# MLP's first slice: weight sums on VectorE fed by GpSimd's DMA queue, the relu's square on ScalarE

## The chip, the cores and the metric

One Trainium2 chip, one core. The metric is the device time of one execution in microseconds. Times quoted as "median" come from three executions; every profile line comes from one profiled execution.

## The reference

One layer of a streaming encoder trunk on 528 tokens (16 meta tokens and 512 of the sequence) of width 1024, all in float32. An input projection feeds a recurrent branch and an attention branch; both are gated, merged and added to `h`. Then follows the part that matters here, on the 512 tokens that are returned:

```python
z = rmsnorm(h, norm_mlp[l])
h = h + (jnp.square(jax.nn.relu(z @ w_up[l])) @ w_down[l])
return h[:, N_META:]
```

`w_up` is 1024 x 4096 and `w_down` 4096 x 1024.

## The kernel before, in words

**Precision.** TensorE multiplies in a reduced float32 format. Each operand is split in a high part (a cast, on ScalarE) and a low part (operand minus high part, on VectorE), and a product is three matmuls: high x high, high x low, low x high (`passes`). So every weight piece that comes from memory (tile `wraw`, 128x512) costs a cast to `whi` on ScalarE and a subtraction to `wlo` on VectorE before TensorE can use it. For the up weights that is `load_h` (L231 the load, L234 the cast, L235 the low part); for the down weights it is `fill`, through `split` (L269, L270). `wraw`, `whi` and `wlo` have four buffers each.

**The MLP.** It starts at 553.7 us of the span. The 4096 hidden units are cut in 32 blocks of 128 and these in four slices of eight blocks. A slice has two stages:

1. The up stage (L1220 to L1236). For each of the eight blocks, 24 matmuls make `po` in PSUM, 128 hidden units by 512 tokens (L1143). `up_evac` takes it out: ScalarE writes relu(po) to `r` (L1149), and VectorE multiplies max(po, 0) by `r` into two of the 256-token columns of `R` (L1150). After every second block, `left_factors` makes the seven left factors of a Strassen-Winograd product from `R`: three subtractions and additions (L1160, L1161, L1162), casts to `fhi` on ScalarE (L1155) and low parts `flo` on VectorE (L1156). Then `factor_sums` makes four sums of down-weight pieces for this pair.
2. The product stage (L1285 to L1309). Seven products (L1256) of left factors with right factors follow. The right factors are plain quarters of `w_down` (B11, B21, B22) or sums of them (T1 to T4). The order of `FACTORS` is B11, B21, T4, T2, T3, T1, B22, so the first sum is read in the third product.

The first slice differs in that the first three blocks' first halves of tokens are multiplied early (`held`), while the last tokens of `z` are still being made.

**The sums.** `factor_sums(p0, j)` loads four pieces of 128x512 (b11, b12, b22, b21) with `quarter`, into the tile `traw` of three buffers, on SyncE's DMA queue (L1176). GpSimd adds them (L1184): T1 = b11 + b12, T3 = b12 + b22, T2 = T1 + b22, T4 = T2 + b21. A slice has 16 such sums, four for each of its four pairs, in tiles `t` that live until that slice's product has read them. SyncE's queue also carries the up weights (L231) and the plain down-weight pieces (also L1176, into `wraw`); it issues in order, and an issue waits until its buffer is free.

**What sets the order.** In the MLP the order of each engine's instructions, and of each DMA queue, is set when the program is built: a scheduler keeps a time for each engine and takes the earliest-written instruction that is ready by its own model. On the chip each engine follows its list in order and waits where an operand is not there.

Of the kernel before, what the change touches and what calls it, by code (L numbers as in the profile page):

```python
# [13 lines left out]
AF = mybir.ActivationFunctionType  # L14
ALU = mybir.AluOpType
# [171 lines left out]
def kernel(ctx, tc, ht, x, win, par, cst, gain, lora, wout, wo, wup, wdn, out, dbg=None):  # L187
    nc = tc.nc
    dbg = dbg or {}
    mm = nc.tensor.matmul  # L190
    act = nc.scalar.activation
    V, G, A = nc.vector, nc.gpsimd, nc.scalar
# [45 lines left out]
    def load_w(src, low=(V, V)):  # L238

        return [load_h(src[:, 512 * j:512 * j + 512], low[j], "w", (4, 4, 4)) for j in range(2)]  # L240
# [31 lines left out]
    def passes(w, x):  # L272
        return ((w[0], x[0]), (w[0], x[1]), (w[1], x[0]))
# [3 lines left out]
    quarters = [[wdn[i][256 * c:256 * c + 256] for c in range(8)] for i in range(4)]  # L277
# [761 lines left out]
    def ppo():  # L1039
        return ps.tile([128, 512], F32, name="po")  # L1040
# [4 lines left out]
    with ExitStack() as st:  # L1045
# [7 lines left out]
        for m in range(KB):  # L1053
            w = load_w(wout[m])
            pp = []
            for br in range(2):
# [3 lines left out]
                po = ppo()  # L1060
# [21 lines left out]
        for j in range(2):  # L1082
            we = yp.tile([128, 2, 2, 512], F32R, name=f"we{j}", tag=("y_rw", "y_fx")[j])
            for x in range(2):
                raw = wp.tile([128, 512], F32, name="wraw", bufs=4)
# [11 lines left out]
        for k in range(KB):  # L1097
            raw = wp.tile([128, 512], F32, name="wraw", bufs=4)
# [9 lines left out]
        for i in range(4):  # L1108
            po = ppo()
# [26 lines left out]
    with ExitStack() as st:  # L1136
        dp = st.enter_context(tc.tile_pool(name="dp", bufs=1))

        def up_part(w, po, t0, t1):
            n = 0  # L1140
            for k in range(KB):
                for a, b in passes(wk(w, k), Z):
                    mm(po[:, t0:t1], a, b[:, k, t0:t1], start=n == 0, stop=n == 23)  # L1143
                    n += 1

        def up_evac(po, out):

            r = dp.tile([128, 512], F32, name="r", bufs=2)
            act(r, po, AF.Relu)  # L1149
            V.scalar_tensor_tensor(out, po.rearrange("p (a b) -> p a b", b=256), 0.0, r.rearrange("p (a b) -> p a b", b=256), ALU.max, ALU.mult)  # L1150

        def left_factors(fhi, flo, j, R):

# [12 lines left out]
        B11, B12, B22, B21, T1, T2, T3, T4 = range(8)  # L1166
# [4 lines left out]

        sums = {}

        def quarter(right, pair, pool=dp, name="traw", bufs=3):
            raw = pool.tile([128, 512], F32, name=name, bufs=bufs)
            nc.sync.dma_start(raw, quarters[right][pair // 2][128 * (pair % 2):128 * (pair % 2) + 128])  # L1176
            return raw

        def factor_sums(p0, j):
            pair = p0 + j  # L1180
            b11, b12, b22, b21 = (quarter(x, pair) for x in (B11, B12, B22, B21))
            for x, c, d in (T1, b11, b12), (T3, b12, b22), (T2, T1, b22), (T4, T2, b21):
                t = dp.tile([128, 512], F32, name=f"t{x}{j}")
                G.tensor_tensor(t, sums[c, pair] if c in (T1, T2) else c, d, ALU.add)  # L1184
                sums[x, pair] = t

        def right_factor(right, pair):
            return sums[right, pair] if (right, pair) in sums else quarter(right, pair, wp, "wraw", 4)

        def fill(n):  # L1190

            while line and len(ready) < n:
                right, p, j = line.pop(0)
                raw = right_factor(right, p + j)
                hi = wp.tile([128, 512], F32R, name="whi", bufs=4)
                lo = wp.tile([128, 512], F32R, name="wlo", bufs=4)
                split(hi, lo, raw)
                ready.append((hi, lo))
# [7 lines left out]
        def soon(*jobs):  # L1206
            later.extend(jobs)

        for p0, n_pairs in zip(FIRST, SLICES):
            fhi = dp.tile([128, max(SLICES), 7, 256], F32R, name="fhi")  # L1210
            flo = dp.tile([128, max(SLICES), 7, 256], F32R, name="flo")
            blocks = list(range(2 * p0, 2 * (p0 + n_pairs)))
            held, R = [], None
            if p0 == 0:

                ws, pos = early + [load_w(wup[2])], [ppo() for i in range(3)]
                for w, po in zip(ws, pos):
                    up_part(w, po, 0, 256)
                held = list(zip(ws, pos))
            for n, b_ in enumerate(blocks):  # L1220
                if held:
                    w, po = held.pop(0)
                    up_part(w, po, 256, 512)
                else:
                    w = load_w(wup[b_])
                    po = ppo()
                    up_part(w, po, 0, 512)
                if n == 2 * n_pairs - 1:
                    fill(AHEAD)
                if n % 2 == 0:  # L1230
                    R = yp.tile([128, 8, 256], F32, name="R", tag=("y_rw", "y_fx")[n // 2 % 2])
                    up_evac(po, R[:, 0:8:7, :])
                else:
                    up_evac(po, R[:, 1:3, :])
                    left_factors(fhi, flo, n // 2, R)
                    factor_sums(p0, n // 2)  # L1236

            first, last = p0 == 0, p0 + n_pairs == 16

            def product(x, left, start, stop, end=False):  # L1240

                for j in range(n_pairs):
                    fill(1)
                    w = ready.pop(0)
                    if later:
                        later.pop(0)()
                    if end and j >= n_pairs - 2:
                        if j == n_pairs - 2:
                            held = w
                            continue  # L1250
                        order = [(i, j + d, (held, w)[d + 1]) for i in range(2) for d in (-1, 0)]
                    else:
                        order = [(i, j, w) for i in range(2)]
                    for i, k, u in order:
                        for n, (a, c) in enumerate(passes((fhi, flo), u)):
                            mm(x[i], a[:, k, left, 128 * i:128 * i + 128], c, start=start and k == 0 and n == 0,  # L1256
                               stop=stop and k == n_pairs - 1 and n == 2)

            def own(left, end=False):
                x = [ppo() for i in range(2)]  # L1260
                product(x, left, True, True, end)
                return x

            def gathered(v, left):
                for i, x in enumerate(own(left)):
                    if first:
                        A.copy(v[:, i], x)
                    else:
                        V.tensor_tensor(v[:, i], v[:, i], x, ALU.add)

            def add(a, b, i, x, op):
                h = hr[a][b][:, i]
                V.tensor_tensor(h, h, x, op)  # L1273

            def store(a, b, i):
                r0 = 256 * a + 128 * i
                nc.sync.dma_start(out[r0:r0 + 128, 512 * b:512 * b + 512], hr[a][b][:, i])

            def added(a, b, left, op, end=False):
                for i, x in enumerate(own(left, end)):  # L1280
                    add(a, b, i, x, op)
                    if end:
                        store(a, b, i)

            gathered(v1, A11)  # L1285
            added(0, 0, A12, ALU.add)
            if last:
                for i in range(2):
                    soon(lambda i=i: (add(0, 0, i, v1[:, i], ALU.add), store(0, 0, i)))
            added(1, 0, A22, ALU.add)  # L1290
            product(x6, S2, first, last)
            if last:
                for i in range(2):
                    V.tensor_tensor(v1[:, i], x6[i], v1[:, i], ALU.subtract)
                    soon(lambda i=i: add(0, 1, i, v1[:, i], ALU.add))
            product(x7, S3, first, last)
            if last:
                for i in range(2):
                    V.tensor_tensor(v1[:, i], v1[:, i], x7[i], ALU.subtract)
                    soon(lambda i=i: (add(1, 0, i, v1[:, i], ALU.subtract), store(1, 0, i)))  # L1300
                for i in range(2):
                    soon(lambda i=i: add(1, 1, i, v1[:, i], ALU.add))
            gathered(v5, S1)
            if last:
                for i in range(2):
                    soon(lambda i=i: add(0, 1, i, v5[:, i], ALU.subtract))
                for i in range(2):
                    soon(lambda i=i: (add(1, 1, i, v5[:, i], ALU.subtract), store(1, 1, i)))
            added(0, 1, S4, ALU.subtract, last)  # L1309
# [77 lines left out]
```

## Time and profile before

| | |
|---|---|
| median of 3 runs | 893.23 us (890.7 to 898.81) |
| profiled execution | 891.46 us, span 889.7 us |
| mean granted TensorE clock | 0.987 |
| up stage of the first slice | 553.7 to 601.4 us |
| its first product stage | from 601.4 us |
| GpSimd's busy time over the span | 246.0 us, in 201 instructions |

A row of a group reads: line, engine, operation, output <- inputs, shapes, count; then busy time and the mean of one in ns; then the engine's idle time before them and what ended it. A row of waits reads: who waited, for whom, us in total, number of times, the longest. A row by windows gives the busy time of each engine and its number of instructions in that stretch, then the granted TensorE clock, the share of the DMA engines and GB/s. A row of the timeline gives start, duration and, in brackets, the engine's idle time before it and what ended it. PE is TensorE, PEld its weight loads, DVE VectorE, ACT ScalarE, POOL GpSimd, SP SyncE; SPq is SyncE's queue of DMA issues.

### The profile page before, as it was taken

Reading aid. Unit: us, or ns where it says so; the run is one execution under the profiler, and the core shown is the slowest. Engines: PE = TensorE matmul, PEld = TensorE weight load, DVE = VectorE, ACT = ScalarE, POOL = GpSimd, SP = SyncE. Lnnn points to the kernel's source line nnn. Section 1 sums busy time; section 2 is a strip of 40 time slices with the busy share of each in tenths; the row PEclk is TensorE's granted clock in tenths of the full one; section 3 lists DMA queues with packets and bytes.
Section 4 is the critical chain, followed back from the end, with each engine's and each line's share of the span. In section 5 each row is a group of like instructions: output and inputs, shape, how many; then the busy total and the mean of one; then the engine's idle time right before and its main releaser. Section 6 shows DMA issues by size and latency. Waiting matters only on the chain. (4 is left out here: it accounts for less than half of the span.)

```text
span 889.7 us, 15657 instructions
## 1 busy us (share of the span) xinstructions
PE 855.4 (96%) x5896; PEld 697.0 (78%) x5896; DVE 632.1 (71%) x1178; ACT 447.9 (50%) x927; POOL 246.0 (28%) x201
## 2 busy tenths in 40 slices
PE   7889899999999999999979999999999999999998
PEld 6878887778896787677758778978888888888886
DVE  6975896547878883565467655598687768877787
ACT  7747333865465533664464553246445434543552
POOL 1154443222353351112102200550640152046000
PEclk9999999999999999999979999999999999999999
DMA  6121114021121241212266550463564175326431
GB/s 215 52 93 48 49 39 150 2 89 56 51 65 52 65 137 56 78 50 72 65 220 196 183 180 11 131 193 91 171 209 108 51 230 159 118 70 226 117 97 71
DMA packets 52363, 95.90 MB, mean 108 GB/s; under 512 B 5816, under 2 KB 6968, under 8 KB 52288
## 3 DMA queue, kind: packets, MB, share of 16 engines
q1 hardware_dynamic: 49984, 90.71, 33.0%
q10 hardware_dynamic: 2304, 4.20, 1.3%
q8 instruction: 46, 0.75, 0.4%
q14 instruction: 29, 0.24, 0.1%
HBM read 88.57 MB, written 6.31 MB: 107 GB/s over the span
## 5 line engine op out<-in xcount | busy, mean ns | idle before, releaser
L497 PE MATMUL pj<-uhi,whi 128*128 128x264 f32 (+1 forms) x480 | 167.3, 348 | 0.0
L497 PE MATMUL pj<-ulo,whi 128*128 128x264 f32 (+1 forms) x480 | 155.6, 324 | 2.4 <-DVE ulo L400 2.4
L467 POOL TENSOR_TENSOR wlo<-wraw,whi 128x512 fp32r<-128x512 f32 x76 | 104.7, 1381 | 191.4 <-ACT whi L466 175.0
L497 PE MATMUL pj<-uhi,wlo 128*128 128x264 f32 (+1 forms) x480 | 155.2, 323 | 0.0
L497 PEld LDWEIGHTS pj<-uhi,whi 128*128 128x128 f32 x480 | 91.4, 191 | 20.4 <-issue 11.3
L1184 POOL TENSOR_TENSOR t<-traw 128x512 f32<-128x512 f32 x32 | 47.0, 1478 | 209.1 <-DVE wlo L270 132.0
L497 PEld LDWEIGHTS pj<-ulo,whi 128*128 128x128 f32 x480 | 91.8, 191 | 7.2 <-DVE ulo L400 2.9
L497 PEld LDWEIGHTS pj<-uhi,wlo 128*128 128x128 f32 x480 | 91.6, 191 | 7.1
L1143 PE MATMUL po<-zhi,wlo 128*128 128x512 f32 (+1 forms) x248 | 95.0, 383 | 1.6 <-DVE wlo L235 1.6
L235 DVE TENSOR_TENSOR wlo<-wraw,whi 128x512 fp32r<-128x512 f32 x88 | 75.8, 874 | 27.7 <-ACT whi L234 27.7
L1143 PE MATMUL po<-zhi,whi 128*128 128x512 f32 (+1 forms) x248 | 94.8, 382 | 0.0
L1143 PE MATMUL po<-zlo,whi 128*128 128x512 f32 (+1 forms) x248 | 94.8, 382 | 0.0
L234 ACT CAST whi<-wraw 128x512 fp32r<-128x512 f32 x88 | 53.5, 618 | 46.3 <-DMA wraw<-in_wup 27.8
L466 ACT CAST whi<-wraw 128x512 fp32r<-128x512 f32 x80 | 49.0, 619 | 41.3 <-PE pj L497 21.0
L1256 PE MATMUL po<-wlo,fhi 128*128 128x512 f32 x160 | 62.8, 392 | 0.2 <-DVE wlo L270 0.2
L1256 PE MATMUL po<-whi,flo 128*128 128x512 f32 x160 | 62.5, 390 | 0.0
L270 DVE TENSOR_TENSOR wlo<-t,whi 128x512 fp32r<-128x512 f32 x64 | 49.3, 784 | 18.5 <-ACT whi L269 17.6
L269 ACT CAST whi<-t 128x512 fp32r<-128x512 f32 x64 | 40.0, 625 | 44.1 <-DVE wlo L270 19.8
L1256 PE MATMUL po<-whi,fhi 128*128 128x512 f32 x160 | 62.0, 389 | 0.0
L1143 PEld LDWEIGHTS po<-zhi,wlo 128*128 128x128 f32 x248 | 46.6, 188 | 11.4 <-DVE wlo L235 2.4
L1143 PEld LDWEIGHTS po<-zlo,whi 128*128 128x128 f32 x248 | 46.6, 188 | 9.1
L1143 PEld LDWEIGHTS po<-zhi,whi 128*128 128x128 f32 x248 | 46.6, 188 | 8.9
(294 smaller groups left out, 1842.2 us busy)
## 6 DMA issues: line engine op xcount, KB each, us to landing
wraw<-in_win SPq DMA_DIRECT2D x84, 256.0 KB, 2.8
wraw<-in_wup SPq DMA_DIRECT2D x64, 256.0 KB, 3.6
traw<-in_wdn SPq DMA_DIRECT2D x64, 256.0 KB, 3.0
wraw<-in_wdn SPq DMA_DIRECT2D x48, 256.0 KB, 2.7
gd<-gt ACTq DMA_DIRECT2D x16, 256.0 KB, 2.0
wraw<-in_wout SPq DMA_DIRECT2D x16, 256.0 KB, 3.1
gl<-gd SPq DMA_DIRECT2D x16, 256.0 KB, 3.0
wraw<-in_wo SPq DMA_DIRECT2D x16, 256.0 KB, 3.0
```

The lines of the kernel that those rows point to most:

```text
L234: A.copy(hi, raw)
L235: low.tensor_tensor(lo, raw, hi.bitcast(F32), ALU.subtract)
L269: A.copy(hi, x)
L270: V.tensor_tensor(lo, x, hi.bitcast(F32), ALU.subtract)
L466: A.copy(hi, raw)
L467: low.tensor_tensor(lo, raw, hi.bitcast(F32), ALU.subtract)
L497: mm(po, a, b[:, k, a0:a1], start=n == 0, stop=n == 23)
L1143: mm(po[:, t0:t1], a, b[:, k, t0:t1], start=n == 0, stop=n == 23)
L1184: G.tensor_tensor(t, sums[c, pair] if c in (T1, T2) else c, d, ALU.add)
L1256: mm(x[i], a[:, k, left, 128 * i:128 * i + 128], c, start=start and k == 0 and n == 0, stop=stop and k == n_pairs - 1 and n == 2)
```

## The change

Only the first slice (`p0 == 0`) is touched, in three ways. Its 16 sums run on VectorE instead of GpSimd. The 16 pieces they read are issued by GpSimd's DMA queue instead of SyncE's; they still share the three `traw` buffers, which slices two to four go on filling from SyncE's queue and reading with GpSimd. And the square in its eight `up_evac` calls is ScalarE's `Square` of `r`, instead of VectorE's product of max(po, 0) with `r`. The values computed are the same.

```diff
-        def up_evac(po, out):
+        def up_evac(po, out, by_act):
 
             r = dp.tile([128, 512], F32, name="r", bufs=2)
             act(r, po, AF.Relu)
-            V.scalar_tensor_tensor(out, po.rearrange("p (a b) -> p a b", b=256), 0.0, r.rearrange("p (a b) -> p a b", b=256), ALU.max, ALU.mult)
+            r = r.rearrange("p (a b) -> p a b", b=256)
+            if by_act:
+                act(out, r, AF.Square)
+            else:
+                V.scalar_tensor_tensor(out, po.rearrange("p (a b) -> p a b", b=256), 0.0, r, ALU.max, ALU.mult)
...
-        def quarter(right, pair, pool=dp, name="traw", bufs=3):
+        def quarter(right, pair, pool=dp, name="traw", bufs=3, queue=nc.sync):
             raw = pool.tile([128, 512], F32, name=name, bufs=bufs)
-            nc.sync.dma_start(raw, quarters[right][pair // 2][128 * (pair % 2):128 * (pair % 2) + 128])
+            queue.dma_start(raw, quarters[right][pair // 2][128 * (pair % 2):128 * (pair % 2) + 128])
             return raw
 
         def factor_sums(p0, j):
             pair = p0 + j
-            b11, b12, b22, b21 = (quarter(x, pair) for x in (B11, B12, B22, B21))
+            eng, queue = (V, G) if p0 == 0 else (G, nc.sync)
+            b11, b12, b22, b21 = (quarter(x, pair, queue=queue) for x in (B11, B12, B22, B21))
             for x, c, d in (T1, b11, b12), (T3, b12, b22), (T2, T1, b22), (T4, T2, b21):
                 t = dp.tile([128, 512], F32, name=f"t{x}{j}")
-                G.tensor_tensor(t, sums[c, pair] if c in (T1, T2) else c, d, ALU.add)
+                eng.tensor_tensor(t, sums[c, pair] if c in (T1, T2) else c, d, ALU.add)
                 sums[x, pair] = t
...
-                    up_evac(po, R[:, 0:8:7, :])
+                    up_evac(po, R[:, 0:8:7, :], p0 == 0)
                 else:
-                    up_evac(po, R[:, 1:3, :])
+                    up_evac(po, R[:, 1:3, :], p0 == 0)
```

## Prediction

> **What bounds the kernel now.** I read the page's busy line first, then the busy times by window around the first slice, then the waits of each engine there, then single instructions.
>
> ```profile
> PE 855.4 (96%) x5896; PEld 697.0 (78%) x5896; DVE 632.1 (71%) x1178; ACT 447.9 (50%) x927; POOL 246.0 (28%) x201
> ```
> ```profile
> core 0: us, PE busy (x) PEld busy (x) DVE busy (x) ACT busy (x) POOL busy (x), PEclk, DMA share, GB/s
> 553.70:567.30 13.60, 13.49 (x113) 13.28 (x113) 3.48 (x5) 3.00 (x7) 4.67 (x4) 1.00 0.31 98
> 567.30:601.40 34.10, 32.54 (x164) 27.28 (x163) 31.25 (x32) 14.57 (x23) 19.52 (x13) 1.00 0.60 177
> 601.40:640.00 38.60, 38.60 (x171) 31.84 (x170) 28.34 (x38) 20.48 (x33) 11.53 (x8) 1.00 0.38 110
> ```
>
> The change acts between 553.7 us, where the first slice's up matmuls begin, and 601.4 us, where its first product begins. TensorE is busy for 13.49 + 32.54 = 46.03 of these 47.70 us, at the full granted clock (1.00), and for all 38.60 us after that. All that any rearrangement here can win is 1.67 us. It is one hole:
>
> ```profile
> PE po L1143 <- DVE wlo L235: 1.6, 1, 1.6
> ```
> ```profile
> 588.77 0.39 PE L1143 MATMUL po<-zlo,whi 128*128 128x512 f32 x1
> 590.72 0.50 PE L1143 MATMUL po<-zhi,wlo 128*128 128x512 f32 x1 [1.56 <-DVE wlo L235]
> ```
>
> Block 6's low half came late. VectorE makes it, and VectorE is the crowded engine of this stretch (31.25 of 34.10 us). Why it is crowded stands in its own rows, beside GpSimd's:
>
> ```profile
> 585.28 1.40 DVE L1161 TENSOR_TENSOR R<-R 128x256 f32<-128x256 f32 x1
> ...
> 587.47 1.51 DVE L1162 TENSOR_TENSOR R<-R 128x256 f32<-128x256 f32 x1
> 588.91 1.76 DVE L235 TENSOR_TENSOR wlo<-wraw,whi 128x512 fp32r<-128x512 f32 x1
> 590.59 2.31 DVE L1156 TENSOR_TENSOR flo<-R,fhi 128x1024 fp32r<-128x1024 f32 x1
> 592.83 0.68 DVE L235 TENSOR_TENSOR wlo<-wraw,whi 128x512 fp32r<-128x512 f32 x1
> ...
> 595.94 0.69 DVE L1160 TENSOR_TENSOR R<-R 128x512 f32<-128x512 f32 x1
> 596.67 0.43 DVE L1161 TENSOR_TENSOR R<-R 128x256 f32<-128x256 f32 x1
> ...
> 597.88 0.42 DVE L1162 TENSOR_TENSOR R<-R 128x256 f32<-128x256 f32 x1
> ...
> 599.42 1.23 DVE L1156 TENSOR_TENSOR flo<-R,fhi 128x1024 fp32r<-128x1024 f32 x1 [0.52 <-ACT fhi L1155]
> ```
> ```profile
> 562.15 2.54 POOL L1184 TENSOR_TENSOR t<-traw 128x512 f32<-128x512 f32 x2 [52.78 <-issue]
> 564.65 1.29 POOL L1184 TENSOR_TENSOR t<-t,traw 128x512 f32<-128x512 f32 x1
> ...
> 587.40 1.31 POOL L1184 TENSOR_TENSOR t<-traw 128x512 f32<-128x512 f32 x1 [1.00 <-DMA traw<-in_wdn]
> 588.66 3.15 POOL L1184 TENSOR_TENSOR t<-t,traw 128x512 f32<-128x512 f32 x2
> ```
>
> The last sum of GpSimd ends at 588.66 + 3.15 = 591.81. Before that the same VectorE shapes cost 1.51, 1.76 and 2.31 us; after it 0.42, 0.68 and 1.23 us. Each is longer by about 1.08 us, a little less than one GpSimd add. So VectorE's two-input operations wait for GpSimd's adds.
>
> [...]
>
> **The change, part by part.** Sixteen sums (four pairs, four each) leave GpSimd, and VectorE's wait for them goes with them. By shape, over the first slice:
>
> ```profile
> L235 DVE TENSOR_TENSOR wlo<-wraw,whi 128x512 fp32r<-128x512 f32 x8 | 10.1, 1288 | 0.0
> L1156 DVE TENSOR_TENSOR flo<-R,fhi 128x1024 fp32r<-128x1024 f32 x3 | 5.8, 1949 | 0.5 <-ACT fhi L1155 0.5
> L1150 DVE SCALAR_TENSOR_TENSOR R<-po,r 128x512 f32<-128x512 f32 x8 | 5.5, 684 | 9.9 <-ACT r L1149 9.9
> ...
> L1161 DVE TENSOR_TENSOR R<-R 128x256 f32<-128x256 f32 x4 | 3.8, 939 | 0.1
> L1160 DVE TENSOR_TENSOR R<-R 128x512 f32<-128x512 f32 x4 | 3.5, 863 | 0.1
> ...
> L1162 DVE TENSOR_TENSOR R<-R 128x256 f32<-128x256 f32 x3 | 2.3, 781 | 0.0
> ```
>
> Against the undisturbed durations above: L235 10.1 − 8 × 0.68 = 4.7; L1156 5.8 − 3 × 1.23 = 2.1; L1161 3.8 − 4 × 0.43 = 2.1; L1160 3.5 − 4 × 0.69 = 0.7; L1162 2.3 − 3 × 0.42 = 1.0. VectorE gets back 10.6 us.
>
> The eight squares (L1150) leave VectorE: 8 × 0.684 = 5.5 us, of which 7 × 0.684 = 4.8 lie before 601.4. The sixteen sums come to it: an add of 128x512 is L1160's 0.69, so 11.0 us. VectorE has nothing to do before 567.32 (9.9 us of idle before L1150), and GpSimd did 3 of its 16 sums by 566; if VectorE does the same three there, 13 × 0.69 = 9.0 fall into the crowded stretch. VectorE's need from 567.3 to 601.4 becomes 31.25 − 10.6 − 4.8 + 9.0 = 24.9 us. With TensorE's hole gone the stretch is 32.5 us long, so VectorE has 7.6 us to spare where it had under 3.
>
> ScalarE takes the squares: 8 × 0.63 by the only 128x512 Square near by.
>
> ```profile
> 554.68 0.63 ACT L1119 ACTIVATE xt<-hres 128x512 f32<-128x512 f32 x1 [2.44 <-DVE hres L1116]
> ```
> ```profile
> ACT fhi L1155 <- DVE R L1150: 8.7, 2, 5.3
> ```
>
> That is 5.0 us more on an engine that is busy 14.57 of 34.10 us: no cost on the path. Its casts for L234 stand in the same queue and will stand 0.63 us later behind a square; but ScalarE itself now makes R, so its 8.7 us of waiting for VectorE's R go, and the casts of block 6 queued behind come sooner. Net I take zero; if ScalarE were full it would cost up to 5.0. No load of an activation table is expected, since Square already runs here beside Ln under one table.
>
> SyncE loses sixteen issues and their waits for GpSimd; the up weights of the later blocks, which stood behind them, can leave as soon as their own buffers are free.
>
> ```profile
> SPq L1176 <- POOL t L1184: 22.4, 16, 2.4
> ```
> ```profile
> 558.36 19.74 SPq L1176 DMA_DIRECT2D traw<-in_wdn  x12
> 578.15 0.42 SPq L231 DMA_DIRECT2D wraw<-in_wup  x1
> ...
> 588.73 3.44 SPq L1176 DMA_DIRECT2D traw<-in_wdn  x3
> 592.26 0.38 SPq L1176 DMA_DIRECT2D wraw<-in_wdn  x1
> ```
>
> The gain of this is inside the 1.67 us. The three pieces issued from 588.73 are already slice two's (12 + 2 + 1 + 1 = 16 came before); they stay on SyncE, wait for the last readers of the shared three buffers, now VectorE's sums, and hold the plain factors of the first product behind them. Sums that end after 591.81 would make that product late.
>
> GpSimd's queue issues the sixteen pieces; nothing else of GpSimd's is due then. The trace has no issue of this kind by GpSimd. From below it is bounded by SyncE's 0.33 us issue, from above by GpSimd's own add of 128x512, 1.30 us; landing by 2.6 to 4.2 us.
>
> ```profile
> L1176 SPq DMA_DIRECT2D traw<-in_wdn x64: 327/328/434, 558.4 to 816.8; - x64
> ...
> DMA to landing us min/median/max: 2.6/3.0/4.2
> ```
>
> I take 1.30, since GpSimd's engine does the work, and the median 3.0. A buffer's round is then 1.30 + 3.0 + 0.69 = 5.0 us; sixteen pieces in three buffers are 5.3 rounds, 26.6 us, from 558.4 to 585.0. That is 6.8 us before GpSimd ended, and 24 us before the first sum is read:
>
> ```profile
> 609.12 0.62 ACT L269 CAST whi<-t 128x512 fp32r<-128x512 f32 x1
> ```
>
> [...]
>
> New is that VectorE waits for pieces, with L235, L1156 and the rest queued behind the waiting sum, and TensorE behind those. Of the rounds, 13/3 = 4.33 lie in the crowded stretch. In each, VectorE has (24.9 − 9.0)/4.33 = 3.7 us of other work against 1.30 + 3.0 = 4.3 us of transfer. Where that work is ordered between the sums it waits 0.6 us a round, 2.6 in all, inside its spare 7.6. Where none is, it waits 4.33 × 4.3 = 18.6 us; with the slowest landing, 4.33 × 5.5 = 23.8.
>
> Sum: −1.67 for the hole; sums, squares, issues and GpSimd's relief at zero, all inside VectorE's and ScalarE's spare time. The profiled execution took 891.46 us (span 889.7), 1.8 below the median of 893.23; it becomes 889.8. On the median's level this is 891.5, which I forecast. What is late next is a piece of the same engine's work, block 7's factor for the first product, by 0.2 us:
>
> ```profile
> PEld po L1256 <- DVE flo L1156: 0.2, 1, 0.2
> ```
>
> **The rivals.** First, slower: VectorE waits in order for pieces of the three buffers. With W us of such waits before 601.4 the change of the time is −1.7 + (W − 7.6). It breaks even at W = 9.3, 2.1 us a round; it reaches +8.9 us (1%) at W = 18.2, 4.2 us a round; its end is W = 23.8, +14.5, thus 907.7. For it speaks that an engine's order is fixed beforehand, with no knowledge of how GpSimd's issues turn out, and that ScalarE's 5.3 us wait for R shows what such an order does to the work behind. Against it, the first round lies in VectorE's idle time, and the evacuation work is there to be put between. Up to break-even it is my forecast; mild (893 to 902) or heavy (902 to 908) beyond.
>
> Second, no change: the hole stays because the cast (L234) or the load of block 6 is as late as VectorE was: 893.2. For it: ScalarE's longer queue. Against it: both lose waits.
>
> Third, GpSimd's issues themselves wait for VectorE: if each of the sixteen waits out one operation of up to 1.23 us, the queue needs 16 × (1.30 + 1.23) = 40.5 us, the last piece is issued at 598.9 and lands at 601.9. The sums still precede 609.12, but slice two's pieces and the plain factors behind them on SyncE go 10 us later than 591.81, against 601.4 when the first is used: up to +9, in the middle 897. The trace has such waits between VectorE and GpSimd's adds only. [...]
>
> **How the numbers follow.** Forecast 0.48 (its own range 889 to 894); mild waits 0.16; heavy waits 0.20; hole stays 0.07; GpSimd's issues held 0.06; a gain beyond 1% 0.03, for which no row gives room, since TensorE has 1.67 us to win. Heavy waits are the slower side, 0.20; the rest but the 0.03 is within 1%, 0.77. One per cent, 8.9 us, is about what a measurement of this kernel can tell from no change: its three runs span 890.7 to 898.81. The range 888.5 to 903 leaves out most of the heavy waits and little below.
>
> **What would show it.** Right: no GpSimd adds before 601; L235, L1161 and L1162 at 0.68, 0.43 and 0.42 throughout; no TensorE idle at block 6; product one about 1.7 us earlier. Waits of VectorE's L1184 for traw over 2.1 us a round, or a last sum after 591.81, prove the first rival; GpSimd issues over 1.3 us apart while VectorE is busy, the third. The forecast is wrong if TensorE's idle time before the first product exceeds 1.7 us.

## The result: 0.3% faster

| | median, us | runs | ratio of after to before |
|---|---|---|---|
| before | 891.97 (889.41 to 898.81) | 20 | |
| after | 889.89 (886.92 to 895.12) | 20 | 0.9968, interval [0.9953, 0.9984] |

The ratio is worth 0.0032 x 892 = 2.9 us, with 1.4 to 4.2 in the interval. The profiled execution of the changed kernel took 888.58 us, span 886.8. It is 2.9 us below that of the kernel before, but not all of this is the change: 0.8 us lie ahead of the MLP, where the same code ran. In the twelve profiles of this study the first up matmul starts anywhere from 551.2 to 557.2 us, though all edits lie behind it. So I read the effect from a stretch that this does not touch: from the first up matmul (row `zhi,we`, the first of its two start times) to the start of the last one (row `zhi,wlo`, the second of its start times). The columns are duration in ns (least, median, most), then first and last start.

Kernel before:

```profile
L1143 PE MATMUL po<-zhi,we x64: 278/283/366, 553.8 to 569.2; 128*128 128x256 f32 x64
...
L1143 PE MATMUL po<-zhi,wlo x248: 283/389/497, 560.9 to 846.6; 128*128 128x512 f32 x116, 128*128 128x256 f32 x8
```

Changed kernel:

```profile
L1143 PE MATMUL po<-zhi,wlo x248: 283/389/390, 560.2 to 843.7; 128*128 128x512 f32 x116, 128*128 128x256 f32 x8
...
L1143 PE MATMUL po<-zhi,we x64: 278/283/367, 553.0 to 568.5; 128*128 128x256 f32 x64
```

The stretch is 846.6 - 553.8 = 292.8 us before and 843.7 - 553.0 = 290.7 after: 2.1 us shorter. In what follows, "stretch" is this number.

Most of it is the hole before block 6, and that cost more than its row says. The prediction shows the matmul ahead of it (588.77 us, in the kernel before) and the one behind it (590.72); the next is this:

```profile
591.06 0.40 PE L1143 MATMUL po<-zhi,whi 128*128 128x512 f32 x1
```

Undisturbed matmuls of this shape start 0.23 us apart (588.54 and 588.77 us just before), though each row lasts 0.39 us. Two starts take 0.46 us, and here they took 591.06 - 588.77 = 2.29: the hole cost 1.83 us where its row says 1.56, so 0.27 more. In e4 (below) a wait of 0.53 us cost 0.8 by the stretch, which agrees.

The busy times of the changed kernel by window, cut at its own first matmul, first square and first product (columns as in the prediction):

```profile
553.00:566.60 13.60, 13.49 (x113) 13.28 (x112) 6.11 (x9) 3.01 (x8) 3.38 (x6) 1.00 0.28 97
566.60:598.70 32.10, 32.10 (x163) 27.41 (x163) 24.63 (x39) 19.30 (x31) 5.37 (x10) 1.00 0.66 199
598.70:640.00 41.30, 41.30 (x184) 34.19 (x183) 28.44 (x38) 21.87 (x36) 12.54 (x9) 1.00 0.39 117
```

TensorE is busy in all of the 32.10 us where it had 32.54 of 34.10. The hole before block 6 is gone. VectorE is busy 24.63 us there and no longer 31.25. Its groups in the first slice (line numbers have moved by four or five) show why:

```profile
L1189 DVE TENSOR_TENSOR t<-t,traw 128x512 f32<-128x512 f32 x8 | 5.5, 690 | 3.3 <-DMA traw<-in_wdn 3.3
L1189 DVE TENSOR_TENSOR t<-traw 128x512 f32<-128x512 f32 x8 | 5.5, 689 | 6.2 <-DMA traw<-in_wdn 6.2
L235 DVE TENSOR_TENSOR wlo<-wraw,whi 128x512 fp32r<-128x512 f32 x8 | 5.3, 684 | 0.0
L1160 DVE TENSOR_TENSOR flo<-R,fhi 128x1024 fp32r<-128x1024 f32 x3 | 3.7, 1223 | 0.5 <-ACT fhi L1159 0.5
...
L1165 DVE TENSOR_TENSOR R<-R 128x256 f32<-128x256 f32 x4 | 1.7, 424 | 0.1
```

The means of L235, of the wide low part and of L1165 (it was L1161) are 684, 1223 and 424 ns, where they were 1288, 1949 and 939. Sixteen sums were added, 11.0 us, and yet VectorE is less busy; of the 6.6 us that it lost in this window, 4.8 are the squares that moved. ScalarE's squares cost what was expected:

```profile
L1152 ACT ACTIVATE R<-r 128x512 f32<-128x512 f32 x8 | 5.1, 632 | 0.2
```

GpSimd now has DMA issues in the first slice's up stage and nothing else. Below are one row for its first three, one for its last, and the group:

```profile
558.20 1.77 POOL L1180 DMA_DIRECT2D traw<-in_wdn  x3 [49.00 <-DVE zlo L1131]
...
585.29 0.54 POOL L1180 DMA_DIRECT2D traw<-in_wdn  x1 [3.54 <-DVE t L1189]
```
```profile
L1180 POOL DMA_DIRECT2D traw<-in_wdn x16: 536/536/707, 558.2 to 585.3; - x16
```

And VectorE's new waits are there, as waits for pieces:

```profile
POOL traw L1180 <- DVE t L1189: 18.7, 10, 3.5
DVE t L1189 <- DMA traw<-in_wdn: 9.5, 8, 3.3
```

Of the 9.5 us, 5.1 lie before the first square (566.6 us) and 4.4 behind it (1.32 + 1.20 + 0.83 + 0.54 + 0.49). TensorE waits for none of them.

### The profile page after: what moved, and what is told of

Same layout as the page of the kernel before. It is cut to its first block, busy times and chain, and to the rows that moved or that the text cites. A ratio compares the mean times of both kernels' runs of the same rounds, so it can differ in the third digit from the quotient of the medians.

```text
span 886.8 us, 15663 instructions
## 1 busy us (share of the span) xinstructions
PE 856.2 (97%) x5896; PEld 698.0 (79%) x5896; DVE 626.4 (71%) x1186; ACT 452.3 (51%) x935; POOL 229.4 (26%) x201
## 4 chain that ended last, share of the span: by engine, by line
PE 76%; DVE 11%; ACT 3%; DMA 3%; issue 2%; POOL 0%; ACTq 0%; DVEq 0%; POOLq 0%
PE pj L497 20%; PE po L1143 20%; PE po L1261 11%; PE pd L1261 5%; PE po L1113 3%; PE po L1064 2%; PE pw L851 1%; DMA gl<-gd 1%; PE psc L603 1%; PE py L648 1%; PE psr L784 1%; DVE L L755 1%; PE pbt L799 1%; PE pssq L549 1%; PE ppt L634 1%
## 5 line engine op out<-in xcount | busy, mean ns | idle before, releaser
L235 DVE TENSOR_TENSOR wlo<-wraw,whi 128x512 fp32r<-128x512 f32 x88 | 74.4, 856 | 27.8 <-ACT whi L234 27.7
L1189 POOL TENSOR_TENSOR t<-traw 128x512 f32<-128x512 f32 x24 | 34.2, 1433 | 155.3 <-DVE wlo L270 138.9
```

What stands on the lines that cost most here:

```text
L235: low.tensor_tensor(lo, raw, hi.bitcast(F32), ALU.subtract)
L1189: eng.tensor_tensor(t, sums[c, pair] if c in (T1, T2) else c, d, ALU.add)
```

## The experiments

Three theories of the hole stood to be told apart. P: VectorE's two-input operations wait for GpSimd's adds (the prediction's). L: VectorE simply had too much work of its own. S: the up weights stood behind the pieces on SyncE's queue.

| run | first slice: sums; pieces' queue; squares | stretch, us | ratio to before, interval |
|---|---|---|---|
| before | GpSimd; SyncE; VectorE | 292.8 | 1 |
| after | VectorE; GpSimd; ScalarE | 290.7 | 0.9968 [0.9953, 0.9984] |
| e1 | GpSimd; GpSimd; VectorE | 295.2 | 1.0009 [0.9986, 1.0032] |
| e2 | GpSimd; SyncE; ScalarE | 292.1 | 0.9978 [0.995, 1.0005] |
| e3 | VectorE; SyncE; ScalarE | 290.6 | 0.9965 [0.9938, 0.9992] |
| e4 | VectorE; GpSimd; VectorE | 291.5 | 0.9951 [0.9931, 0.997] |
| e5 | e3, and GpSimd adds that nobody reads | 298.5 | 1.0042 [1.0025, 1.0059] |
| e6 | e3, and GpSimd fills with zeros | 290.7 | 0.9959 [0.9933, 0.9984] |
| e7 | after, with two buffers of their own for the pieces | 300.6 | 1.0077 [1.005, 1.0103] |
| e8 | the change in all four slices | 292.2 | 0.999 [0.9967, 1.0014] |

The intervals of e1, e2 and e8 contain 1, and they are too wide to order e2, e3, e4 and after among themselves; for that the stretch and the waits in it are used, from one profile of each kernel. The scheduler lays out each kernel anew, so each run differs from its neighbour in the order of some instructions too.

**Both kernels again**, to see how far one profile repeats.

> The kernel before, unchanged, once more, to see how far one profile repeats. If the stretch from the first to the last up matmul is set by the order of the instructions alone, it is 292.8 us within 0.2 again, with one TensorE wait of 1.5 to 1.7 us before block 6; the first up matmul starts anywhere from 552 to 557.5 us, as in the runs so far. If the stretch itself varies by over 0.5 us, gains of 0.7 and 1.3 us read from single profiles can't be told apart.

> The changed kernel, unchanged, once more: the stretch 290.7 us within 0.2 and no TensorE wait before the first product, if the order sets it; otherwise as for c1_before_again.

The stretches are 292.8 and 290.6 us, from first up matmuls at 554.5 and 551.2 us; the single times were 892.09 and 886.7 us. So the stretch repeats within 0.1 us in both pairs, and I read differences of 0.2 us and more from one profile of each kernel.

**e1, the queue alone.**

```diff
-            eng, queue = (V, G) if p0 == 0 else (G, nc.sync)
+            eng, queue = (G, G) if p0 == 0 else (G, nc.sync)
-                    up_evac(po, R[:, 0:8:7, :], p0 == 0)
+                    up_evac(po, R[:, 0:8:7, :], False)
```

(and the same in the other call of `up_evac`.)

> Only the queue of the first slice's pieces moves to GpSimd; its sums stay on GpSimd, its squares on VectorE. Theory P (VectorE's two-input operations wait for GpSimd's adds, and that opens TensorE's hole before block 6): the adds are still there, so VectorE's L235, L1156 and L1161 stay about 1.1 us longer beside them, the hole of 1.5 to 2 us stays, time within 1 us of before. Theory S (the up weights stood behind the pieces on SyncE's queue): hole gone, 1.7 to 2 us faster.

The stretch is 2.4 us longer than before. TensorE's waits, then VectorE's low parts, then GpSimd's last sums:

```profile
PE po L1143 <- DVE wlo L235: 1.7, 3, 0.9
PE po L1261 <- DVE flo L1160: 0.6, 1, 0.6
PE po L1261 <- ACT fhi L1159: 0.5, 1, 0.5
```
```profile
L235 DVE TENSOR_TENSOR wlo<-wraw,whi 128x512 fp32r<-128x512 f32 x8 | 11.2, 1425 | 0.0
```
```profile
594.86 3.44 POOL L1189 TENSOR_TENSOR t<-t,traw 128x512 f32<-128x512 f32 x2
```

Freeing SyncE's queue alone won nothing, which speaks against S. GpSimd's issues now stand between its adds, the sums end 43.3 us behind the first up matmul and no longer 38.0, and the interference reaches into the first product. By the stretch this is slower than P's "within 1 us" too; P has the mechanism, and the delay of the adds by the issues had not been counted. TensorE now waits five times (2.83 us by the rows) where it waited once (1.56). That is 1.3 us more; the other 1.1 are, by estimate, the four further waits, each at the 0.27 us that the hole above cost beyond its row.

**e2, the squares alone.**

```diff
-            eng, queue = (V, G) if p0 == 0 else (G, nc.sync)
+            eng, queue = G, nc.sync
```

> Only the first slice's squares move to ScalarE; sums stay on GpSimd, pieces on SyncE. VectorE's need falls by 4.8 us, from 31.25 to 26.5 of 32.5 us, and its waits for GpSimd stay. Theory L (VectorE had simply too much work): hole gone, 1.7 to 2 us faster. Theory P: the waits of 10.6 us stay, at least 0.5 us of the hole stays, gain 0 to 1.2 us. Theory S: no change.

The stretch is 0.7 us shorter than before, and the hole is still there, smaller:

```profile
PE po L1143 <- DVE wlo L235: 1.0, 1, 1.0
```

This is P's outcome, not L's: 4.8 us less work make the hole smaller, but do not close it while VectorE's operations stay stretched (L235's mean here is 1228 ns).

**e3, the change without its queue.**

```diff
-            eng, queue = (V, G) if p0 == 0 else (G, nc.sync)
+            eng, queue = (V, nc.sync) if p0 == 0 else (G, nc.sync)
```

> The change without its move of the queue: sums on VectorE, squares on ScalarE, the pieces stay on SyncE's queue ahead of up weights. Theories P and L: hole gone, 1.7 to 2 us faster, as the whole change. Theory S: the hole stays, no change.

The stretch is 290.6 us, and the only TensorE wait is the 0.2 us that every kernel has at its end. The pieces stand ahead of the up weights on SyncE's queue again, and the hole is gone all the same: S falls. The move of the queue is worth nothing here.

**e4, the change without the squares.**

```diff
-                    up_evac(po, R[:, 0:8:7, :], p0 == 0)
+                    up_evac(po, R[:, 0:8:7, :], False)
```

(and the other call.)

> The change without the move of the squares: sums on VectorE, pieces from GpSimd's queue, squares on VectorE as before. VectorE's need is 24.9 + 4.8 = 29.7 of 32.5 us, plus the 4.4 us that it waited for pieces after 567.3 in the changed kernel: 34.1, about what it had before. Theory L: hole of 1 to 2 us stays, time within 1 us of before. Theory P: no operation of VectorE is stretched, and no hole or one under 0.5 us: 1.2 to 2 us faster.

Block 6 waits no more; block 7's factor is late for the first product:

```profile
PE po L1261 <- DVE flo L1160: 0.5, 1, 0.5
PE po L1261 <- DVE wlo L270: 0.2, 1, 0.2
```

The stretch is 291.5: 1.3 us of the 2.1 come from moving the sums, and the squares bring the last 0.8. P is confirmed as the main part; L has a share in what comes next.

**e5 and e6, GpSimd's work given back.** Both start from e3. The spent tile `r` is used after each square, so that both are paced by the blocks and hold the same buffers.

```diff
                 act(out, r, AF.Square)
+                for _ in range(2):
+                    G.tensor_tensor(r, r, r, ALU.add)
```
```diff
                 act(out, r, AF.Square)
+                for _ in range(5):
+                    G.memset(r, 0.0)
```

> e3_sync_queue, and after each of the first slice's eight squares GpSimd adds the spent tile r to itself twice (16 adds of 128x512 that nobody reads, as many as it had in the kernel before). Measured by the stretch from the first up matmul to the start of the last one in the profile, 292.8 us before and 290.6 in e3_sync_queue. Theory P (VectorE's two-input operations wait for GpSimd's adds): VectorE's operations beside them are again up to 1.1 us longer, TensorE waits again for a low part in the first slice, 0.5 to 3 us, stretch 291.1 to 294. Theory L (amount of VectorE's own work): no wait, 290.6.

> As e5_gp_reads, but GpSimd fills r with zeros five times after each square in place of the two adds: about as long busy, writing only. If VectorE waits for GpSimd's reads alone: no operation of VectorE is longer, no TensorE wait in the first slice, 290.6 us. If it waits for any GpSimd operation: as e5_gp_reads, 291.1 to 294.

GpSimd's group, VectorE's R <- R of 128x512 (4 of them in the first slice) and L235, in e5:

```profile
L1154 POOL TENSOR_TENSOR r<-r 128x512 f32<-128x512 f32 x16 | 23.5, 1477 | 74.5 <-DVE t L1191 59.1 <-ACT R L1152 14.8
```
```profile
L235 DVE TENSOR_TENSOR wlo<-wraw,whi 128x512 fp32r<-128x512 f32 x8 | 7.0, 893 | 0.0
...
L1166 DVE TENSOR_TENSOR R<-R 128x512 f32<-128x512 f32 x4 | 5.3, 1314 | 0.0
```

The same in e6:

```profile
L1154 POOL MEMSET r<- 128x512 f32 x40 | 21.0, 526 | 74.1 <-ACT R L1152 72.3
```
```profile
L235 DVE TENSOR_TENSOR wlo<-wraw,whi 128x512 fp32r<-128x512 f32 x8 | 5.4, 686 | 1.2 <-ACT whi L234 1.2
...
L1166 DVE TENSOR_TENSOR R<-R 128x512 f32<-128x512 f32 x4 | 2.8, 688 | 0.9 <-ACT R L1152 0.9
```

GpSimd is about as long busy in both, and in neither does ScalarE wait for GpSimd to release `r`. With adds, VectorE's operations beside them are stretched (R <- R at 1314 ns against 688, L235 at 893 against 686) and TensorE waits; with fills, no group of them is, and the stretch is 290.7. So these two-input operations of VectorE wait for GpSimd's adds, and not for GpSimd being busy or writing. Not every two-input operation does: the squares of the kernel before, which read `po` and `r`, took 0.68 to 0.69 us also beside adds:

```profile
569.15 2.55 POOL L1184 TENSOR_TENSOR t<-traw 128x512 f32<-128x512 f32 x2 [1.44 <-DMA traw<-in_wdn]
...
576.18 3.26 POOL L1184 TENSOR_TENSOR t<-traw 128x512 f32<-128x512 f32 x2 [1.08 <-DMA traw<-in_wdn]
```
```profile
570.15 0.69 DVE L1150 SCALAR_TENSOR_TENSOR R<-po,r 128x512 f32<-128x512 f32 x1 [2.14 <-ACT r L1149]
...
576.51 0.68 DVE L1150 SCALAR_TENSOR_TENSOR R<-po,r 128x512 f32<-128x512 f32 x1
```

An add reads and a fill does not; that the reading is the reason, and not the adding itself, no run here separates.

The size in e5 was missed: 5.7 us longer than before, where at most 1.2 was expected. Its waits are longer than expected, and they do not explain it alone:

```profile
PE po L1263 <- DVE flo L1162: 3.0, 1, 3.0
PE po L1143 <- DVE wlo L235: 1.4, 1, 1.4
```

With the 0.2 us at the end these are 4.6 us, 2.8 more than the 1.8 before. Nearly all of the other 2.9 us follow the 3.01 us wait:

```profile
603.75 0.39 PE L1263 MATMUL po<-wlo,fhi 128*128 128x512 f32 x1
607.15 0.80 PE L1263 MATMUL po<-whi,flo 128*128 128x512 f32 x1 [3.01 <-DVE flo L1162]
607.75 0.63 PE L1263 MATMUL po<-whi,fhi 128*128 128x512 f32 x1
608.17 0.63 PE L1263 MATMUL po<-wlo,fhi 128*128 128x512 f32 x1
608.60 0.63 PE L1263 MATMUL po<-whi,flo 128*128 128x512 f32 x1
```
```profile
608.00:610.00 2.00, 2.00 (x6) 1.52 (x6) 1.78 (x3) 1.73 (x4) 0.00 (x0) 0.50 0.47 116
610.00:612.00 2.00, 2.00 (x6) 1.54 (x5) 0.69 (x1) 0.49 (x2) 0.00 (x0) 0.50 0.41 151
612.00:614.00 2.00, 2.00 (x8) 1.61 (x7) 0.69 (x1) 0.59 (x2) 0.00 (x0) 0.71 0.48 131
614.00:616.00 2.00, 2.00 (x10) 1.63 (x9) 0.74 (x2) 1.16 (x2) 0.00 (x0) 1.00 0.00 0
```

Behind the wait the matmuls start 0.43 us apart and not 0.23, at a granted clock of 0.50, until about 613 us: some 14 of them at 0.2 us each, 2.8 us.

**e7, two buffers.** The price of VectorE's waits, the prediction's first rival, by dose. The two buffers are a tile of their own (`trav`), so slice two's pieces no longer share buffers with these.

```diff
-            b11, b12, b22, b21 = (quarter(x, pair, queue=queue) for x in (B11, B12, B22, B21))
+            b11, b12, b22, b21 = (quarter(x, pair, queue=queue, **({"name": "trav", "bufs": 2} if p0 == 0 else {})) for x in (B11, B12, B22, B21))
```

> The changed kernel with two buffers of their own for the first slice's pieces instead of three. Sixteen pieces then need 8 rounds and not 5.3, so VectorE waits longer for them. First rival of the prediction (time = -1.7 + W - 7.6, W the waits after the first evacuation): W grows from 4.4 us by 2.7 rounds of about 3.5 us to some 14, and the stretch is 4 to 5 us longer than before, 297. If the order puts other work between: W below 7.6 and 290.7 as in the changed kernel.

```profile
DVE t L1189 <- DMA trav<-in_wdn: 21.3, 11, 5.9
```
```profile
PE po L1261 <- DVE flo L1160: 2.5, 1, 2.5
PE po L1261 <- DVE wlo L270: 1.2, 2, 1.0
PE po L1261 <- ACT whi L269: 1.0, 1, 1.0
PE po L1143 <- DVE wlo L235: 0.6, 1, 0.6
```

Of these waits for pieces (first row) 12.5 us lie between 567.3 us, where the prediction began to count, and the first product at 600.8 us (eight waits in the timeline, the first counted from 567.3 us on; 0.9 to 2.7 us each). By the prediction's formula that is -1.7 + 12.5 - 7.6 = 3.2 us slower; TensorE's waits are 5.3 us in sum, 3.5 more than before. The stretch is 7.8 us longer, where 4 to 5 were expected. Most of the other 4.3 us are again matmuls at half the clock. They begin after two waits of 1.0 us each within 4 us, and again after the wait of 2.5:

```profile
603.49 0.50 PE L1261 MATMUL po<-whi,fhi 128*128 128x512 f32 x1 [0.99 <-ACT whi L269]
605.02 0.50 PE L1261 MATMUL po<-wlo,fhi 128*128 128x512 f32 x1 [1.03 <-DVE wlo L270]
...
606.38 0.63 PE L1261 MATMUL po<-whi,fhi 128*128 128x512 f32 x1
606.80 0.63 PE L1261 MATMUL po<-wlo,fhi 128*128 128x512 f32 x1
...
612.40 0.50 PE L1261 MATMUL po<-whi,flo 128*128 128x512 f32 x1 [2.54 <-DVE flo L1160]
```
```profile
606.00:609.00 3.00, 3.00 (x9) 2.29 (x9) 2.50 (x4) 2.01 (x4) 0.54 (x1) 0.53 0.66 201
```

In both places together some 15 matmuls start 0.43 us apart, 3.0 us in all; three waits more than before, by estimate at the 0.27 us each that the hole cost above its row, make 0.8; half a microsecond is left unexplained. So the rival's mechanism is real and its formula comes near TensorE's waits (3.2 against 3.5), but it leaves out the clock of 0.53 that followed two of these waits.

**e8, all four slices.**

```diff
-            eng, queue = (V, G) if p0 == 0 else (G, nc.sync)
+            eng, queue = V, G
-                    up_evac(po, R[:, 0:8:7, :], p0 == 0)
+                    up_evac(po, R[:, 0:8:7, :], True)
```

(and the other call.)

> The change in all four slices: all 64 sums on VectorE from GpSimd's queue, all 32 squares on ScalarE. TensorE has no hole in slices two to four (0.2 us), so by theory P there is nothing more to win: 290.7 us as in the changed kernel, although VectorE's operations there get shorter too. Rival: VectorE's in-order waits for pieces open new holes in the later slices, 1 to 5 us longer.

```profile
DVE t L1189 <- DMA traw<-in_wdn: 34.1, 31, 3.4
```
```profile
PE po L1261 <- DVE wlo L270: 1.5, 2, 1.3
```

The stretch is 292.2: 1.5 us longer than with the first slice alone, the rival's outcome. The later slices had no hole to close, and VectorE's waits for their pieces opened one of 1.3 us at 718 us: VectorE stood idle for 2.62 us until a piece came at 715.93 us, and the low part that TensorE needed came behind that sum, from 717.73.

## Why the prediction was right, step by step

- **The hole as all there is to win: right, the size a little short.** 1.67 us were forecast, 2.1 came off the stretch. From the first up matmul to the first product the timelines have 47.64 us before and 45.67 after, 2.0 less; the first product itself lost less than 0.1, so block 7's factor, named as late next, cost next to nothing. The term was short because the hole cost 1.83 us where its row says 1.56.
- **The level: off by its base.** 891.5 us were forecast and 889.89 measured. The forecast was put on the three-run median of 893.23, which twenty runs put at 891.97; 1.3 of the 1.6 us between come from there and not from the change.
- **VectorE's stretched operations: right, mechanism and size.** 10.6 us were to come back; L235, L1165 and the wide low part run at 684, 424 and 1223 ns. e5 and e6 show that GpSimd's adds are the cause (R <- R at 1314 ns beside adds, 688 beside fills).
- **VectorE's balance: right.** Its need was put at 24.9 us of 32.5; it was busy 24.63 of 32.10.
- **The squares at no cost: right.** 0.63 us each, ScalarE busy 19.30 us; both profiles have 11 loads of an activation table, none of them behind 553 us; and e4 shows that without their move 0.8 of the 2.1 us would be missing, which the prediction had not separated.
- **SyncE's relief inside the gain: right.** e3 has the hole closed without it, and e1, which has it alone, won nothing.
- **GpSimd's issue: mis-sized.** It was taken as 1.30 us between 0.33 and 1.30; it is 0.54. A piece lands in 3.1 us (median of the sixteen), where 3.0 was taken.
- **The round of a buffer: mis-sized the other way.** 5.0 us were forecast, an end of the sums at 585.0; the last sum ended at 588.43 + 0.69 = 589.1, so a round took 5.8. Issue, landing and sum make 0.54 + 3.1 + 0.69 = 4.3 us of that; the other 1.5 lie between them, where a landed piece waits for VectorE to come to its sum, or for the other piece. It cost nothing: the sums are first read more than 15 us later, and VectorE's 4.4 us of waits stayed inside the 7.6 to spare.
- **Rivals.** The first did not come with three buffers; e7 shows that it comes with two, and there at its mild size (12.5 us of waits, between the 9.3 and 18.2 of the prediction). The second is excluded by the hole's absence. The third did not come: all issues took 0.54 to 0.71 us while VectorE was busy. The sign named for it, issues over 1.3 us apart, was no good sign: they are up to 4.07 us apart (572.98 and 577.05 us), but the rows give a buffer not yet free as what GpSimd waited for.

Heavy waits, at a chance of 0.20 more likely than mild ones at 0.16, did not come even with one buffer less; one outcome does not say more of a chance. Of the kernels tried, none beats the changed one by more than can be measured: with TensorE without a wait from the first up matmul to the first product, the first slice's up stage has no more to give.

## What to carry to other kernels

When an engine looks too full, compare the same shape's duration beside another engine's work and away from it: here some 10.6 of VectorE's 34.7 busy us in the first up stage were waiting for GpSimd's adds, and taking these over at half their price (0.69 us against 1.30) did not make VectorE busier (32.9 us in e4, with one square of 0.7 us fewer in the window). What such a change could win here was about the idle time of the engine that bounds the stage (1.67 us idle, 2.1 won); apply it where that idle time is (here one slice of four) and leave it elsewhere. An in-order engine that is fed by a short ring of buffers needs its spare time counted against the sum of its waits, and one buffer decided the sign here: against 292.8 us before, the stretch was 290.7 with three buffers and 300.6 with two.

## What the runs showed of the hardware that was not expected

A DMA issue by GpSimd costs it 0.54 us here for a piece of 128x512 float32, against SyncE's 0.33. It hardly stretched beside a busy VectorE: the sixteen took 0.54 to 0.71 us while VectorE was busy for 24.63 of 32.10 us.

TensorE's waits had a second price in two runs, beyond the 0.27 us that the hole cost above its row. Single waits of 1.34 (e8), 1.38 (e5) and 1.56 us (before), and five of at most 0.9 spread over the up stage and the product (e1), left the granted clock at 1.00. One of 3.01 us (e5) was followed by matmuls at a granted clock of 0.50 (608 to 612 us), and two of 0.99 and 1.03 us within 4 us (e7) by matmuls at 0.53 (606 to 609 us). Behind a later one of 2.54 (e7) the clock was 0.62 in the mean of 612 to 616 us. These slow matmuls were worth some 2.8 us more in e5 and 3.0 in e7. In e7 no single wait between the first up matmul and the first slow one was longer than 1.03 us. Where the limit lies between these cases was not tried.
